# Small per-channel vectors and all constants issued from GpSimd's queue, behind a marker for the first products' input

## The chip, the cores and the metric

The kernel runs on one core of a Trainium2 chip. The metric is the device time of one launch in microseconds (us); the times shown are medians over several runs. A profiled execution gives the rows quoted below; its span reaches from the first to the last instruction.

Engines are named as the profile names them: PE is TensorE (PEld its weight loads), DVE is VectorE, ACT is ScalarE, POOL is GpSimd, SP is SyncE. A name with a q behind it (SPq, POOLq, ACTq) is the part of an engine that issues DMAs. SP and ACT issue on hardware queues, POOL on a software queue, and all of them use the same 16 DMA engines.

## The reference

256 tokens of 1024 features go through two models in a row: one hybrid layer (attention, a pooling branch, gates, a gated feed-forward with a convolution), and then two layers of latent attention and a mixture of 16 experts. Only the very start of the first one matters here:

```python
def hybrid_layer(x, norm_mix_g, w_in, b_gate, q_norm_g, k_norm_g, w_pool, pool_scale, ...):
    h = rmsnorm(x, norm_mix_g)
    proj = h @ w_in                                   # [256, 1024] @ [1024, 4096]
    q, k, v, u_pool, gate_logits = jnp.split(proj, ...)
    q = apply_partial_rotary(rmsnorm(heads(q), q_norm_g), pos)
    k = apply_partial_rotary(rmsnorm(heads(k), k_norm_g), pos)
    attn = moba_attention(q, k, heads(v))
    pooled = multiscale_pool_mixer(u_pool, w_pool, pool_scale)
    gates = jax.nn.sigmoid(gate_logits + b_gate)
    ...
    up = causal_depthwise_conv(h2 @ w_up, conv_w, conv_b)
```

The vectors q_norm_g, k_norm_g, pool_scale, b_gate, norm_ffn_g, conv_b, conv_w and their like of the later layers are the small loads that the change is about.

## The kernel before

**Products.** Every float32 matrix product is made of three products of parts: a weight or an input is split into a high and a low part (`split`, L84), the high part on ACT (L92), the low part, source minus high, on DVE (L82). A contraction step of 128 rows of w_in against 1024 of its columns is called a k here. It takes 12 matmuls of 512 columns on PE (two halves of the tokens, two halves of the columns, three products). w_in is cut into four column groups c of eight k each; the first two groups (`tm_mm`, L296 on) put tokens on partitions.

**Weight loads.** SP issues the loads of the weights in the order of their use (L137, L158 on): first the two halves of x, with the two halves of in00 between and behind them, then in01, in02, in03, in10, in11 and so on. A tile in`cu` of 1 MB (1024 KB) holds two k of group c. The tiles lie in a ring of 56 KB per partition, which holds seven of them; the eighth may be issued once the first has been split. Behind in11 SP issues 17 loads of small vectors into the tile `rows` (`add_rows`, L145; `load_rows`, L150), from 1 to 22 KB each, and only then in12.

**Lanes.** A DMA signals its landing on one of eight semaphores of its kind of queue (DMAHW0 to DMAHW7 for the hardware queues, DMASW0 to DMASW7 for POOL's). The issue of a DMA waits until the one eight before it on the same kind of queue has landed, and what stands behind it on the issuing engine waits as well.

**Constants.** POOL builds the identity for transposes, and issues 11 loads of constants, 1.7 MB in all: `at` (672 KB, what the attention needs), `bw` (q_norm_g and k_norm_g, each broadcast to 128 partitions, the rotary table, `band` of 544 KB, w_pool of 256 KB), `upb`, `cr`, `rbias` and `rw` for the experts. They don't wait for any computation, so they are issued from the first microseconds on.

**The first products.** x is transposed on PE (`x_rows`, L214), scaled and split to `hh` and `hl` (ACT L221, DVE L222), one k after the other; `keep_warm` (L97) puts transposes without use into waits of PE. ACT and DVE split the weights two k ahead of the products. After four k of the second group, `qk_norm` (L342) normalizes and rotates q and k: DVE multiplies by the row scales (L352), POOL multiplies by `qkg` (L354), DVE rotates (L359 to L364). After six k, four transposes on PE bring `rows` onto partitions (L526).

**Order.** Within an engine a planner sets the order, starting from the program's order; `tc.issue_after` holds instructions behind another one.

Of the kernel before, what the change touches and what calls it, by code (L numbers as in the profile page):

```python
# [10 lines left out]
F32 = mybir.dt.float32  # L11
# [6 lines left out]
PSUM = bass.MemoryType.PSUM  # L18

T = 256  # L20
# [10 lines left out]
# Scores of a head: 128 queries with 128 keys, then 128 queries with all 256 keys.  # L31
# [3 lines left out]
def body(tc, a, out, dbg=None, upto=None):  # L35
# [9 lines left out]
    def A(name, shape=(128, 512)):  # L45
        """One bank of PSUM."""
        return psum.tile(list(shape), F32, tag="A", name=name, bufs=4)

    def H(name, shape=(128, 2, 512)):
        """Two banks of PSUM."""  # L50
        return psum.tile(list(shape), F32, tag="H", name=name, bufs=2)
# [16 lines left out]
    def pin(i):  # L68
        """Keeps an instruction in the order of the program on its engine."""
        return tc.keep_in_program_order(i)  # L70

# [12 lines left out]
    def split(raw, shape=(1024,), eng=None, tile_=hl8, scale=1.0):  # L84
        """raw = hi + lo, both exact in float32r."""
# [11 lines left out]
    def keep_warm(n, dst):  # L97
        """Without work the clock of the tensor engine falls to half: this bridges a wait."""
# [5 lines left out]
    def after(i, col):  # L104
        """behind[i] = 1, once col is there: keeps an operation scaled by it behind col."""
        ve.tensor_scalar(behind[:, i:i + 1], col, 1.0, 1.0, op0=ALU.max, op1=ALU.min)

    def table(func, col):
        """Loads the table of a function, once col is there."""
        se.activation(warm[:, 1:2], col, func, scale=0.0, bias=epsc[0:1, 0:1])  # L110

# [29 lines left out]
    # rows of per-channel vectors, put on partitions by the tensor engine  # L141
# [3 lines left out]
    def add_rows(key, src, b, r):  # L145
        sy.dma_start(rows[n_row[b]:n_row[b] + r, b], src.rearrange("(r c) -> r c", c=128))
# [17 lines left out]
    for c in range(4):  # L164
        for u in range(4):
# [7 lines left out]
            if (c, u) == (1, 2):  # L173
                load_rows()
# [24 lines left out]
    def pre(seq, i, ahead=2, scale=1.0):  # L199
        """Keeps the splits of the units in seq up to i + ahead issued."""  # L200
# [32 lines left out]

    vec = const.tile([128, 86], F32, name="vec")
    v0 = [sum(n_row[:b]) for b in range(4)]
# [15 lines left out]
    class at:  # L251
        """What only the attention needs (and the convolution, at first): a tile for each layer."""
# [14 lines left out]
    bw = act("bw", shape=(128, 2048))  # L267
    band, wpool = (bw[:, o:o + 4 * n].rearrange("p (g c) -> p g c", g=4) for o, n in ((0, 272), (1088, 128)))
    qkg = bw[:, 1600:1728].rearrange("p (i c) -> p i c", i=2)
    cs1 = bw[:, 1728:1760].rearrange("p (t i c) -> p t i c", t=2, i=2)  # L270
    ge.dma_start(qkg[:, 0], a["q_norm_g"].partition_broadcast(128))
    ge.dma_start(qkg[:, 1], a["k_norm_g"].partition_broadcast(128))
    ge.dma_start(cs1, a["c_rot1"])
# [6 lines left out]
    # the last rows come a second time, as the router takes 32 columns at once and drops 16  # L280
# [3 lines left out]
    ge.dma_start(rw[:, KD * 16:], rsrc[:, 0])  # L284

# [7 lines left out]
    def tm_mm(c, acc, k):  # L293
# [3 lines left out]
        if c == k == 0:  # L297
            # the low part of the weights comes last
# [20 lines left out]
    for k in range(KD):  # L319
# [4 lines left out]
        if k == 3:  # L324
            # statistics of the norm, and the vectors that come later
# [52 lines left out]
    def softmax_heads(S, n_, scale, nscale, values, hi, lo):  # L378
        """Scores of two heads, a bank each, to attention outputs with features on partitions."""
# [74 lines left out]
    def fm_out(units, xh, xl, evac, then=None):  # L454
        """8 feature tiles [128, 256] in 4 banks; units: (weight name, row) per contraction tile."""
# [101 lines left out]
    def up_split(i, ss=(0, 1)):  # L557
        """hi and lo of the weights of tile pair i, gate and value."""
# [942 lines left out]
```

## Time and profile before

| What | us |
|---|---|
| Median of the timed runs (3) | 1088.08 |
| Lowest and highest of them | 1087.83, 1089.63 |
| Span of the profiled execution | 1082.4 |
| Median less that span (what lies around the span) | 5.7 |
| PE busy in the span | 1034.8 (96%) |
| DVE, ACT, POOL busy | 540.0, 427.3, 80.4 |

For the profiled execution the page gives the span and no other time, so the 5.7 us are the difference to the median of other executions. PE's busy time is modelled: its 96% say that PE has work nearly all the time, not that it runs at its peak. The chain of waits is the better guide to what sets the end, and for a change at the start of the program the time line of the first 60 us.

### The profile page before, as it was taken

How to read it: one execution, taken by the hardware profiler on the slowest of the kernel's cores; microseconds unless marked ns; L12 is line 12 of the kernel's file. 1: busy time of each engine (PE TensorE's matmuls, PEld its weight loads, DVE VectorE, ACT ScalarE, POOL GpSimd, SP SyncE). 2: the span in 40 equal slices, each digit the busy share in tenths (PEclk: the TensorE clock that was granted, in tenths of full speed). 3: DMA queues.
4: the chain of work that ended last, by engine and by line, in shares of the span. 5: the costliest groups of instructions: out<-in, count | busy, mean ns of one | idle time of the engine just before them, and what ended most of it. 6: DMA issues, size and time to landing. Idle time of an engine off the chain costs nothing.

```text
span 1082.4 us, 16579 instructions
## 1 busy us (share of the span) xinstructions
PE 1034.8 (96%) x6732; PEld 738.8 (68%) x6732; DVE 540.0 (50%) x1026; ACT 427.3 (39%) x795; POOL 80.4 (7%) x70
## 2 busy tenths in 40 slices
PE   7999999999999999999999999989999999999994
PEld 5889999999999999765343444368977534343431
DVE  3875578977777689753110111058985402011103
ACT  4766547755554565542110111156654302011111
POOL 3200021000000130010000000044000200000001
PEclk9999999999999999999999999999999999999997
DMA  9752555765443244978999999955297899999993
GB/s 320 307 183 79 208 185 173 256 203 184 156 143 142 83 159 141 352 279 311 397 394 394 396 399 395 377 201 197 79 338 283 315 381 394 398 399 400 395 387 121
DMA packets 131484, 295.08 MB, mean 273 GB/s; under 512 B 5754, under 2 KB 34744, under 8 KB 125128
## 3 DMA queue, kind: packets, MB, share of 16 engines
q1 hardware_dynamic: 130328, 290.58, 72.8%
q0 software_dynamic: 768, 2.84, 0.8%
q8 instruction: 55, 0.90, 0.3%
q10 hardware_dynamic: 304, 0.53, 0.1%
q14 instruction: 29, 0.24, 0.1%
HBM read 291.82 MB, written 2.10 MB: 272 GB/s over the span
## 4 chain that ended last, share of the span: by engine, by line
PE 79%; DVE 11%; DMA 4%; ACT 3%; issue 2%; SPq 0%; POOL 0%; DVEq 0%; ACTq 0%; POOLq 0%
PE gu L74 19%; PE up L74 12%; PE pd L74 10%; PE fm L74 7%; PE yT L74 5%; PE wo L74 5%; PE sc L74 4%; PE tm L74 4%; PE prj L74 3%; PE pg L74 3%; PE sum L74 3%; DVE hl L82 2%; PE sc L399 1%; DMA e<-in_w_down_dram 1%; DMA in<-in_w_in_dram 1%
## 5 line engine op out<-in xcount | busy, mean ns | idle before, releaser
L74 PE MATMUL gu<-e,xg 128*64 128x512 f32 x1024 | 224.2, 593 | 0.0
L74 PEld LDWEIGHTS gu<-e,xg 128*64 128x64 f32 x1024 | 72.3, 137 | 140.1 <-issue 131.5
L74 PE MATMUL up<-h2h,hl 128*128 128x256 f32 x704 | 130.5, 283 | 0.0
L1295 DVE SCALAR_TENSOR_TENSOR sg<-gu,gcol,sg 128x512 f32<-128x512 f32 x16 | 12.0, 751 | 227.5 <-PE gu L74 162.7
L74 PE MATMUL pd<-e,aT 128*64 128x512 f32 x512 | 115.9, 596 | 4.7 <-ACT aT L1305 2.7
L74 PEld LDWEIGHTS up<-h2h,hl 128*128 128x128 f32 x704 | 111.4, 192 | 0.0
L74 PE MATMUL up<-h2l,hl 128*128 128x256 f32 x352 | 99.7, 283 | 0.1
L74 PEld LDWEIGHTS pd<-e,aT 128*64 128x64 f32 x512 | 35.5, 137 | 73.5 <-issue 64.6
L74 PEld LDWEIGHTS up<-h2l,hl 128*128 128x128 f32 x352 | 67.6, 192 | 0.3 <-DVE h2l L515 0.3
L74 PE MATMUL yT<-ac,hl 128*128 128x256 f32 x528 | 67.0, 283 | 0.1
L74 PEld LDWEIGHTS yT<-ac,hl 128*128 128x128 f32 x528 | 64.9, 192 | 0.3 <-ACT ac L635 0.3
L82 DVE TENSOR_TENSOR hl<-up,hl 128x1024 fp32r<-128x1024 f32 x44 | 53.8, 1225 | 19.5 <-ACT hl L92 19.4
L1288 ACT ACTIVATE sg<-gu 128x512 f32<-128x512 f32 x16 | 9.6, 597 | 128.4 <-PE gu L74 128.4
L92 ACT ACTIVATE hl<-up 128x1024 fp32r<-128x1024 f32 x44 | 46.1, 1052 | 33.9 <-PE up L74 28.4
L1323 ACT ACTIVATE y<-pd 128x512 fp32r<-128x512 f32 x32 | 18.2, 597 | 104.1 <-PE pd L74 78.9
L82 DVE TENSOR_TENSOR y<-pd,y 128x512 fp32r<-128x512 f32 x32 | 21.3, 687 | 62.6 <-ACT y L1323 62.5
L74 PE MATMUL fm<-hh,hl 128*128 128x256 f32 x256 | 49.2, 288 | 0.9 <-ACT vu L316 0.9
L74 PE MATMUL tm<-hl,hh 128*128 128x512 f32 x128 | 41.6, 407 | 4.2 <-ACT hl L92 2.4
L1088 DVE TENSOR_SCALAR xg<-pg,vec 128x256 f32<-128x256 f32 x32 | 15.9, 538 | 59.4 <-PE sum L74 44.2
L82 DVE TENSOR_TENSOR hl<-in,hl 128x1024 fp32r<-128x1024 f32 x32 | 38.3, 1220 | 13.9 <-ACT hl L92 13.7
L1222 ACT ACTIVATE GT<-pgt 128x256 fp32r<-128x256 f32 x16 | 6.2, 384 | 95.7 <-PE pgt L1220 95.7
L74 PE MATMUL prj<-xhn,hl 128*128 128x256 f32 x208 | 40.2, 287 | 3.8 <-DVE iq L82 2.6
(354 smaller groups left out, 2052.4 us busy)
## 6 DMA issues: line engine op xcount, KB each, us to landing
e<-in_w_up_dram SPq DMA_DIRECT2D x48, 1024.0 KB
e<-in_w_down_dram SPq DMA_DIRECT2D x48, 1024.0 KB
e<-in_w_gate_dram SPq DMA_DIRECT2D x40, 1024.0 KB
e<-in_w_gate_dram SPq DMA_DIRECT2D x48, 512.0 KB
up<-in_w_up_dram SPq DMA_DIRECT2D x22, 1024.0 KB
e<-in_w_up_dram SPq DMA_DIRECT2D x32, 512.0 KB
e<-in_w_down_dram SPq DMA_DIRECT2D x32, 512.0 KB
in<-in_w_in_dram SPq DMA_DIRECT2D x15, 1024.0 KB
```

The source lines that it names most:

```text
L74: return te.matmul(o, lhsT=l, rhs=r, start=start, stop=stop, skip_group_check=True)
L82: return (eng or ve).tensor_tensor(out=dst, in0=src, in1=hi.bitcast(F32), op=ALU.subtract)
L92: se.activation(hi, raw, AF.Copy, scale=scale)
L399: te.transpose(S[:, i, 128 * b:128 * b + 128], P[:, i, 128 * b:128 * b + 128], ident)
L1088: ve.tensor_scalar(dst, src, g, b, op0=ALU.mult, op1=ALU.add)
L1222: se.activation(GTs[p], pt, AF.Copy)
L1288: se.activation(sg, psg, AF.Silu)
L1295: ve.scalar_tensor_tensor(out=sg, in0=psu, scalar=gcol[:, p:p + 1], in1=sg, op0=ALU.mult, op1=ALU.mult)
L1323: se.activation(h_, pd[c], AF.Copy)
```

## The change

`add_rows` issues on POOL (`ge`) instead of SP. A marker is put on POOL, a copy of one element of `hh` of k = 3 into the tile `warm`, and all of POOL's DMAs of constants and vectors are to be issued after it. Their order is new: q_norm_g, k_norm_g, the rotary table, then the 17 vectors of `rows`, then `at`, `band`, w_pool, `upb`, `cr`, `rbias`, `rw`. The rest of the diff takes comments away, and moves the lines that create the tile `bw` ahead of those that create `at`.

```diff
     def add_rows(key, src, b, r):
-        sy.dma_start(rows[n_row[b]:n_row[b] + r, b], src.rearrange("(r c) -> r c", c=128))
+        ge.dma_start(rows[n_row[b]:n_row[b] + r, b], src.rearrange("(r c) -> r c", c=128))
...
-            if (c, u) == (1, 2):
-                load_rows()
             load(f"in{c}{u}", w_in[u * 256:(u + 1) * 256, c * 1024:(c + 1) * 1024]
...
     x_rows(0)
 
+    mark = ge.tensor_copy(warm[0:1, 2:3], hh[0:1, 3, T - 1:].bitcast(F32))
+    behind_x = ctx.enter_context(ExitStack())
+    behind_x.enter_context(tc.issue_after(mark.ins))
+
     vec = const.tile([128, 86], F32, name="vec")
+    bw = act("bw", shape=(128, 2048))
+    band, wpool = (bw[:, o:o + 4 * n].rearrange("p (g c) -> p g c", g=4) for o, n in ((0, 272), (1088, 128)))
+    qkg = bw[:, 1600:1728].rearrange("p (i c) -> p i c", i=2)
+    cs1 = bw[:, 1728:1760].rearrange("p (t i c) -> p t i c", t=2, i=2)
+    ge.dma_start(qkg[:, 0], a["q_norm_g"].partition_broadcast(128))
+    ge.dma_start(qkg[:, 1], a["k_norm_g"].partition_broadcast(128))
+    ge.dma_start(cs1, a["c_rot1"])
+    load_rows()
...
     attention_tile(ge)
-    bw = act("bw", shape=(128, 2048))
...
-    ge.dma_start(qkg[:, 0], a["q_norm_g"].partition_broadcast(128))
-    ge.dma_start(qkg[:, 1], a["k_norm_g"].partition_broadcast(128))
-    ge.dma_start(cs1, a["c_rot1"])
     ge.dma_start(band, a["c_band"])
...
     ge.dma_start(rw[:, KD * 16:], rsrc[:, 0])
+    behind_x.close()
```

On POOL, at the start of the program and before the change, the loads of constants stand among the instructions that build the identity, and wait for nothing or, from the ninth on, for a lane:

```order
L122 CAST identb<-ident 128x128 [waits Pool_49]
L124 TENSOR_SCALAR alphaI<-ident 128x128
L248 DMA rbias<-in_router_bias_dram 128x16
L283 DMA rw<-in_router_w_dram 128x8x16
L284 DMA rw<-in_router_w_dram 128x16
L256 DMA at<-in_c_att_dram 128x1344
L271 DMA bw<-in_q_norm_g_dram 128x64
L272 DMA bw<-in_k_norm_g_dram 128x64
L273 DMA bw<-in_c_rot_dram 128x32 [waits DMASW0_49]
```

The same place with the change:

```order
L122 CAST identb<-ident 128x128 [waits Pool_49]
L124 TENSOR_SCALAR alphaI<-ident 128x128
L232 COPY warm<-hh 1x1 [waits Activation_49]
L241 DMA bw<-in_q_norm_g_dram 128x64
L242 DMA bw<-in_k_norm_g_dram 128x64
L243 DMA bw<-in_c_rot_dram 128x32
L146 DMA rows<-in_b_gate_dram 16x128
L146 DMA rows<-in_pool_scale_dram 4x128
```

The copy that waits for ACT now stands ahead of every load on POOL, and the `rows` loads have come to POOL, where they number 17 of 28 DMAs.

Further down on POOL, behind the last constants and up to its first work for `qk_norm`, before:

```order
L271 DMA bw<-in_q_norm_g_dram 128x64
L272 DMA bw<-in_k_norm_g_dram 128x64
L273 DMA bw<-in_c_rot_dram 128x32 [waits DMASW0_49]
L274 DMA bw<-in_c_band_dram 128x1088 [waits DMASW1_49]
L275 DMA bw<-in_w_pool_dram 128x4x128 [waits DMASW2_49]
L354 TENSOR_TENSOR qk<-qk,bw 128x512 [waits DMASW6_49,DVE_49,Activation_49]
```

and with the change:

```order
L146 DMA rows<-in_ln_b_dram 8x128 [waits DMASW3_49]
L266 DMA at<-in_c_att_dram 128x1344 [waits DMASW4_49]
L277 DMA bw<-in_c_band_dram 128x1088 [waits DMASW5_49]
L278 DMA bw<-in_w_pool_dram 128x4x128 [waits DMASW6_49]
L258 DMA upb<-in_c_up_dram 128x256 [waits DMASW7_49]
L258 DMA cr<-in_c_route_dram 128x100 [waits DMASW0_49]
L258 DMA rbias<-in_router_bias_dram 128x16 [waits DMASW1_49]
L286 DMA rw<-in_router_w_dram 128x8x16 [waits DMASW2_49]
L287 DMA rw<-in_router_w_dram 128x16 [waits DMASW3_49]
L358 TENSOR_TENSOR qk<-qk,bw 128x512 [waits DVE_49,Activation_49]
```

Of the 28 DMAs the last 20 now wait for a lane, in three rounds of eight, eight and four, and POOL's multiplication by `qkg` stands behind them all.

On SP, behind in11 (in_99), the first load of `rows` stood before and the weights go on now; before:

```order
L138 DMA in_97<-in_w_in_dram 128x2x1024 [waits DMAHW0_49]
L138 DMA in_99<-in_w_in_dram 128x2x1024 [waits DMAHW1_49]
L146 DMA rows<-in_b_gate_dram 16x128 [waits DMAHW2_49]
L146 DMA rows<-in_pool_scale_dram 4x128 [waits DMAHW3_49]
L146 DMA rows<-in_norm_ffn_g_dram 8x128 [waits DMAHW4_49]
```

and with the change:

```order
L138 DMA in_97<-in_w_in_dram 128x2x1024 [waits DMAHW0_49]
L138 DMA in_99<-in_w_in_dram 128x2x1024 [waits DMAHW1_49]
L138 DMA in_101<-in_w_in_dram 128x2x1024 [waits DMAHW2_49]
L138 DMA in_103<-in_w_in_dram 128x2x1024 [waits DMAHW4_49,DMAHW3_49,DVE_49]
L138 DMA in_105<-in_w_in_dram 128x2x1024 [waits DMAHW5_49,DVE_49,Activation_49]
```

in12 (in_101) follows in11 directly, 17 DMAs earlier in SP's order. On PE the order of the instructions is unchanged over the whole program. On ACT and DVE the splits of in03 to in11 and the statistics of the first norm change places with each other, behind the split of in03; from the second column group on their order is unchanged too.

## Rows read from the trace of the kernel before

**Rows 1.** The page: the chain that ended last, shares of the span by engine.
```profile
PE 79%; DVE 11%; DMA 4%; ACT 3%; issue 2%; SPq 0%; POOL 0%; DVEq 0%; ACTq 0%; POOLq 0%
```

**Rows 2.** The chain that ended last, in time: start us, us, what.
```profile
2.72 14.31 DMA in<-in_w_in_dram
...
707.85 10.78 DMA uv<-in_w_uv_dram
...
947.43 14.85 DMA e<-in_w_down_dram
```

**Rows 3.** Stretches: PE, PEld, DVE, ACT, POOL busy, PE's granted clock, DMA, GB/s.
```profile
13.50:16.00 2.50, 2.22 (x10) 1.49 (x8) 0.00 (x0) 0.00 (x0) 0.00 (x0) 1.00 1.01 124
16.00:18.00 2.00, 0.00 (x0) 0.00 (x0) 0.00 (x0) 0.94 (x1) 0.00 (x0) 1.00 0.98 390
...
19.99:23.40 3.41, 3.41 (x10) 2.64 (x9) 1.47 (x2) 0.85 (x1) 0.00 (x0) 0.50 1.02 394
23.40:36.00 12.60, 12.60 (x57) 10.43 (x56) 10.89 (x13) 11.73 (x18) 0.00 (x0) 1.00 0.54 186
```

**Rows 4.** Time line 10 to 20 us: start, us, engine, line, instruction [idle before, releaser].
```profile
10.46 1.15 ACT L92 ACTIVATE hl<-in,behind 128x1024 fp32r<-128x1024 f32 x1 [1.30 <-DMA in<-in_w_in_dram]
...
11.66 0.50 PE L74 MATMUL tm<-hl,hh 128*128 128x512 f32 x1
...
14.18 0.62 PE L74 MATMUL tm<-hl,hh 128*128 128x512 f32 x2
...
14.88 0.62 PE L74 MATMUL tm<-hl,hh 128*128 128x512 f32 x2
...
17.06 2.00 ACT L92 ACTIVATE hl<-in 128x1024 fp32r<-128x1024 f32 x2 [5.09 <-DMA in<-in_w_in_dram]
...
19.42 0.50 PE L74 MATMUL tm<-hl,hh 128*128 128x512 f32 x1 [0.76 <-DVE hl L82]
```

**Rows 5.** DMA queues, 0 to 6 us: packets, MB, share; q1 is SP's, q0 POOL's.
```profile
q1 hardware_dynamic: 462, 1.14, 59.2%
q0 software_dynamic: 31, 0.07, 3.7%
```

**Rows 6.** DMA queues, 10 to 13 us.
```profile
q0 software_dynamic: 138, 0.65, 53.4%
q1 hardware_dynamic: 134, 0.55, 46.5%
```

**Rows 7.** DMA queues, 23 to 27 us, when POOL's loads are over.
```profile
DMA packets 424, 1.64 MB, mean 411 GB/s; under 512 B 23, under 2 KB 23, under 8 KB 424
```

**Rows 8.** POOL's own time line, 0 to 60 us.
```profile
6.21 0.90 POOL L271 DMA_DIRECT2D bw<-in_q_norm_g_dram  x1
7.10 0.54 POOL L272 DMA_DIRECT2D bw<-in_k_norm_g_dram  x1
...
45.47 5.95 POOL L354 TENSOR_TENSOR qk<-qk,bw 128x512 f32<-128x512 f32 x4 [35.08 <-DVE qk L352]
```

**Rows 9.** DMA issues, 0 to 60 us: size, us from issue to landing.
```profile
bw<-in_w_pool_dram POOLq DMA_DIRECT2D x1, 256.0 KB, 13.2
...
upb<-in_c_up_dram POOLq DMA_DIRECT2D x1, 64.0 KB, 5.2
rw<-in_router_w_dram POOLq DMA_DIRECT2D x1, 64.0 KB, 7.2
```

**Rows 10.** SP's time line, 0 to 60 us.
```profile
33.65 24.87 SPq L138 DMA_DIRECT2D in<-in_w_in_dram  x10
```

**Rows 11.** DVE's time line, 0 to 70 us, and PE's at 54 us.
```profile
6.30 0.69 DVE L230 CAST hl<-in 128x1024 fp32r<-128x1024 f32 x1 [5.37 <-DMA in<-in_w_in_dram]
...
51.89 1.21 DVE L82 TENSOR_TENSOR hl<-in,hl 128x1024 fp32r<-128x1024 f32 x1
...
53.80 0.57 PE L526 MATMUL pr<-ident,rows 72*128 72x72 f32 x4
...
54.49 0.70 PE L74 MATMUL tm<-hl,hh 128*128 128x512 f32 x2
```

More of the change, by code (lines that the diff above doesn't have):

```diff
@@ L251, in body @@
     class at:
+        pass
     def attention_tile(eng):
@@ L266, in body @@
     attention_tile(ge)
-    bw = act("bw", shape=(128, 2048))
-    band, wpool = (bw[:, o:o + 4 * n].rearrange("p (g c) -> p g c", g=4) for o, n in ((0, 272), (1088, 128)))
-    qkg = bw[:, 1600:1728].rearrange("p (i c) -> p i c", i=2)
-    cs1 = bw[:, 1728:1760].rearrange("p (t i c) -> p t i c", t=2, i=2)
-    ge.dma_start(qkg[:, 0], a["q_norm_g"].partition_broadcast(128))
-    ge.dma_start(qkg[:, 1], a["k_norm_g"].partition_broadcast(128))
-    ge.dma_start(cs1, a["c_rot1"])
     ge.dma_start(band, a["c_band"])
```

## The prediction

> **What bounds the kernel now.** I read the chain of waits first. Nearly four fifths of it lie on PE, and only 4% on DMAs [rows 1]; of that the longest single piece stands at the very start, 14.31 us until 17.03 for a load of w_in [rows 2]. The change touches nothing behind the first 60 us (PE's order is the same throughout), so the question is how early PE gets into its steady run, and whether anything in those 60 us then stops it. The second view is the time line of 10 to 20 us [rows 4]. The second half of in00 reaches ACT at 10.46, after 1.30 us of waiting; in01 reaches it at 17.06, after 5.09 us of waiting. Between the two PE has one k of work, from 11.66 on, and then none: from 16 to 18 us it is busy 0.00 [rows 3]. Its steady run begins with the second product of the next k at 19.42, which waited for the low part of in01 [rows 4]. The third view is the table by stretches: from 19.99 to 23.40 the granted clock is 0.50, that is 1.2 GHz instead of 2.4, right behind the empty stretch; from 23.40 on it is 1.00 again [rows 3]. From there PE has no gap that matters; whatever it gains before 23.40 should move the whole rest.
>
> Why is in01 late? The queues tell. Until 6 us SP's queue has moved 1.14 MB and POOL's 0.07 MB [rows 5]. From 10 to 13 us POOL's queue has moved 0.65 MB and SP's 0.55 [rows 6]: the constants took more than half of the traffic just when in01 was due. From 13.5 to 16 only 124 GB/s were moved at all, against 390 behind it [rows 3] and 411 when SP is alone [rows 7]. The constants that POOL loads there are needed from 45.47 us on (`qkg`) [rows 8], or much later.
>
> **The change part by part.**
>
> *The constants leave the first 13 us.* By the end of in01 SP's queue has to move x (two times 512 KB), in00 and in01 (1024 KB each): 3.15 MB. 1.14 are there at 6 us; the other 2.01 MB at 411 GB/s [rows 7] take 4.9 us, and I add 0.35 us for the last engine and the landing: in01 at about 11.25 us instead of 17.03, and in00's second half, 1.05 MB earlier, at 8.7. Now what is late next? ACT, which was free for the split of in00 at 10.46 - 1.30 = 9.16, does it then, 1.3 us earlier [rows 4]. PE doesn't profit at once: its first product of that k at 11.66 stands behind transposes and the products of the k before, which start from in00's first half, and that lands at 6.3 either way [rows 11]. But the low part is there by then (9.16 + 1.15 + 1.23 = 11.5), so that the 12 products run through. Three take 14.88 - 14.18 = 0.70 us at most [rows 4], so twelve take 2.75: until 14.4. The split of in01 starts on ACT at 11.3 (1.05 us a k) and its low part on DVE ends by 11.3 + 1.05 + 1.2 = 13.6, before 14.4. So PE's second product of that next k comes at about 14.4 + 0.23 = 14.6 instead of 19.42: **4.8 us**.
>
> *The clock.* The stretch of 3.41 us at half clock [rows 3] does work worth 1.7 us at full clock. It stands behind 2 us without any work, and that gap closes; from 13.5 to 16 us, with PE at work for 2.22 of 2.50 us, the clock was still full [rows 3]. I take the whole gain, **1.7 us**; its lower bound is 0.
>
> *The marker.* It waits for `hh` of k = 3, which ACT writes behind the splits of in01: 11.3 + 2 x 1.05 + 0.45 = 13.9 us. Behind it on POOL stand 28 DMA issues and then the multiplication by `qkg`. The same bytes as before now run beside in02, in03 and in10. in02 is due at 11.25 + 1.05 MB / 411 GB/s = 13.8, before them. in03 would come at 16.4; with 2.5 us for a slow stretch like that of 13.5 to 16, and half of the traffic for POOL, at some 21.5. PE needs its first k at 14.4 + 4 x 2.75 = 25.4, so ACT must have it by 23.1. Cost taken: nothing; up to 1 us if in02 slips.
>
> *POOL's chain of lanes.* An issue takes 0.54 us, or 0.90 in the worst row [rows 8]. Eight issues go out at once, and each further one waits until the one eight before it has landed. With a time L from issue to landing POOL is free at 13.9 + 3 x (0.54 + L) + 4 x 0.54 = 17.7 + 3 L. The trace has small loads at 5.2 and 7.2 us, and 13.2 for one that stood behind `at` [rows 9]. In the new order the first 20 are small and have nothing large ahead of them on their queue, and the last four wait only for small ones; so I take L = 6, and POOL is free at 35.7. It is needed at 45.47 - 6.5 = 39.0. Hidden, by 3 us. If that cover goes, DVE waits with its rotation, and behind it stands the low part for k = 6 of the second group, which ended at 51.89 + 1.21 = 53.1, with PE's first use at 54.49: 1.4 us more. The transposes of `rows` at 53.80 [rows 11], then at 47.3, need the twentieth load, landed by 13.9 + 3 x (0.54 + 6) + 2.2 = 35.7.
>
> *SP without the 17 loads.* in12 was issued at 33.65 [rows 10], and comes some 27 us earlier in the queue. PE didn't wait for it before, so this gains nothing; it gives the ring a lead that pays for POOL's traffic. The identity is ready earlier too, as no DMA issue stands among its steps; in00 covers that.
>
> Sum: 4.8 + 1.7 = 6.5 us off the 1082.4 us of the profiled span. The timed median lies 5.7 us over it, and nothing in that part changes: 1088.1 - 6.5 = **1081.6 us**.
>
> **Against a rule.** The rows show two queues that share the traffic almost evenly [rows 6]. The Trainium skill, page "DMA: Bandwidth & Descriptors", section "Issuing engines are not separate DMA queues", says that DMAs of all issuing engines interleave on the same 16 DMA engines, and that spreading them saves only issue time. The trace agrees with the interleaving. By that rule alone, the bytes being the same, moving `rows` to POOL gives nothing, and the sum would be 1088; my 6.5 us come from the later time of the constants. The same page, section "SWDGE vs HWDGE vs iDMA", says that DVE can lock GpSimd out of the descriptor rings it writes. The 0.90 us issue did lie on DVE's CAST of 6.30 to 6.99, and the next one, beside a TENSOR_TENSOR, took 0.54 [rows 8, 11]; at 0.90 throughout POOL would be free at about 38, still in time.
>
> **The rivals.**
> (a) *Half the gain.* The clock falls all the same in some other stretch, or in01 comes 1 to 2 us later than 11.25 because something other than POOL's loads slowed SP's queue: 6.5 - 1.7 = 4.8, or 6.5 - 1.7 - 1.5 = 3.3 us off, so 1083.3 to 1084.8. For it: the first 6 us move 1.14 MB only, with hardly any of POOL's bytes in them. Against: at 6 us the rate is up.
> (b) *No change.* The collision only moves: the slow stretch hits in02 and in03 instead of in01, PE runs dry at k = 4, the clock falls there. in02 would have to land after 22; with SP's own loads first in line I don't see how, unless the marker comes before in01. A later DMA-bound piece could also eat the gain: 10.78 us at 707.85 and 14.85 at 947.43 [rows 2]; but those loads are issued when PE and DVE free their space, so they move with PE. 1086 to 1090.
> (c) *Slower.* POOL's lanes. PE stands still once POOL is later than 39.0 + 1.4 = 40.4, that is from L = 7.6 on. At L = 9.8 (POOL free at 47.1) the gain is used up, and from there every us of L costs 3. With 13.2 us, the slowest row [rows 9], POOL is free at 57.3, 16.9 late: 1088.1 - 6.5 + 16.9 = 1098.5. For it: the queues are full at that time, and the two broadcasts stand first. Against: 13.2 belongs to a load behind 1.2 MB on its own queue.
> That the marker fails to hold the loads is excluded by the order on POOL.
>
> **How the numbers follow.** Forecast 0.70, (a) 0.13, (b) 0.08, (c) 0.09, of which a third costs so little that it stays faster or equal. What a measurement here can tell from no change is 0.2%, 2.2 us: faster means under 1085.9. Faster: 0.70 + 0.12 + 0.01 = 0.83; same: 0.10; slower: 0.07. The range takes the forecast with 1.6 us below it (the terms at their best, in01 no bound at all), and (a) above it: 1080.0 to 1085.0; (b) and (c) stay outside.
>
> **What would show it.** In the trace after: ACT's two splits of in01 at 11 to 12 us; PE without an empty stretch from 11.66 on; the granted clock at 1.00 through 30 us; the first DMA issue on POOL at about 14; POOL's multiplication by `qkg` at 39, waiting for DVE and not for a DMA; the transposes of `rows` at 47; the whole later chain 6.5 us earlier. It is wrong if ACT waits for in02 or in03 for more than 2 us, if POOL's last issue comes after 40, or if DVE's rotation waits for POOL for longer than before.

## The result, and the profile after

| What | before | after |
|---|---|---|
| Median, us (lowest to highest) | 1088.04 (1087.83 to 1089.63) | 1079.5 (1079.11 to 1080.01) |
| Ratio, 95% interval | | 0.9932 [0.9913, 0.9951] |
| Span of the profiled execution, us | 1082.4 | 1077.6 |
| Time of that same execution, us | not given | 1079.35 |

Faster, by 8.5 us. The forecast was 1081.6 with a range from 1080.0 to 1085.0: the sign, and about three quarters of the size; the time came out half a microsecond below the range. Two later measurements of the same two programs gave 0.996 [0.9945, 0.9975] and 0.9928 [0.9907, 0.9949]; in the three groups the medians lie 8.5, 5.3 and 7.3 us apart, so the first shows the largest gain of the three. The forecast's ratio, 1081.6 / 1088.1 = 0.994, lies inside two of the three intervals. Over all 16 executions the changed kernel's median is 1079.65; over all 91 of the kernel before it is 1087.11, 7.5 us more.

Stretches of [rows 3], in the profile of after (busy us of PE, PEld, DVE, ACT, POOL, then PE's granted clock, DMA share, GB/s), with one more, from 18.5 to 20.5 us:

```profile
13.50:16.00 2.50, 2.50 (x13) 2.06 (x12) 2.42 (x4) 2.50 (x6) 1.67 (x4) 1.00 1.03 410
18.50:20.50 2.00, 2.00 (x11) 1.65 (x10) 2.00 (x4) 1.48 (x4) 0.67 (x2) 1.00 1.12 210
19.99:23.40 3.41, 3.41 (x17) 2.82 (x16) 3.41 (x5) 1.49 (x2) 1.71 (x4) 1.00 0.96 349
23.40:36.00 12.60, 12.24 (x54) 9.72 (x53) 8.59 (x9) 12.24 (x17) 9.18 (x17) 1.00 1.03 398
```

In these stretches PE has no empty time to speak of any more and no half clock (1.2 GHz instead of 2.4, which the profile writes as 0.50); the DMA engines move 410 GB/s where 124 were moved before. The slow spell has not vanished: it moved to 18.5 to 20.5 us, when the two broadcasts, issued at 14.46 and 15.23, are under way, and in02 and in03 are through. From 10 to 13 us SP's queue now has the engines to itself (packets, MB, share; compare [rows 6]):

```profile
q1 hardware_dynamic: 319, 1.24, 102.7%
```

The time line of after, with the rows that answer to [rows 4], [rows 8] and [rows 11] (start, us, engine, line, instruction, idle before and its releaser):

```profile
9.39 1.15 ACT L92 ACTIVATE hl<-in,behind 128x1024 fp32r<-128x1024 f32 x1 [0.36 <-DMA in<-in_w_in_dram]
11.90 2.01 ACT L92 ACTIVATE hl<-in 128x1024 fp32r<-128x1024 f32 x2 [0.99 <-DMA in<-in_w_in_dram]
14.33 0.18 POOL L232 COPY warm<-hh 1x1 f32<-1x1 f32 x1 [12.14 <-ACT hh L219]
14.46 0.78 POOL L241 DMA_DIRECT2D bw<-in_q_norm_g_dram  x1
14.55 0.61 PE L74 MATMUL tm<-hl,hh 128*128 128x512 f32 x2
17.27 0.61 PE L74 MATMUL tm<-hl,hh 128*128 128x512 f32 x2
33.48 0.73 PE L74 MATMUL tm<-hl,hh 128*128 128x512 f32 x2 [0.35 <-ACT qk L320]
34.55 0.55 POOL L287 DMA_DIRECT2D rw<-in_router_w_dram  x1
39.57 5.94 POOL L358 TENSOR_TENSOR qk<-qk,bw 128x512 f32<-128x512 f32 x4 [4.48 <-DVE qk L356]
...
47.90 0.57 PE L530 MATMUL pr<-ident,rows 72*128 72x72 f32 x4
```

in01 reaches ACT at 11.90 instead of 17.06. The marker passes at 14.33, POOL's last issue ends at 35.10, and POOL then waits 4.48 us for DVE: the chain of lanes is hidden. The products of the k behind in01's first start at 17.27. In the profile of before that row is

```profile
23.63 0.63 PE L74 MATMUL tm<-hl,hh 128*128 128x512 f32 x2
```

so PE is 6.36 us ahead there. At 33.48 PE waits for ACT, as it didn't before, and the lead falls from 6.39 to 5.91; the transposes of `rows` come at 47.90 instead of 53.80, 5.90 us earlier. In the chain of waits the first long piece is still a load of w_in, and a longer one than in [rows 2]:

```profile
4.50 15.80 DMA in<-in_w_in_dram
```

It is now the stream of weights itself, which ends at 20.30 with in10, at 410 GB/s in the stretch before the slow spell. Part of the 5.90 us is lost again much later in this execution. From 176 to 180 us the granted clock is 0.57, behind a spell in which PE is not quite busy:

```profile
174.00:176.00 2.00, 1.81 (x15) 1.64 (x16) 1.20 (x3) 1.28 (x3) 0.00 (x0) 1.00 0.52 211
176.00:180.00 4.00, 4.00 (x23) 4.00 (x22) 3.59 (x5) 2.70 (x4) 0.00 (x0) 0.57 0.28 72
```

PE's last products start at 1064.62 instead of 1069.01, so that 4.4 us are left of the 5.90.

### The profile page after: what moved, and what is told of

The parts are those of the page before. It is cut to its first block, busy times and chain, and to the rows that moved or that the text cites. A ratio compares the mean times of both kernels' runs of the same rounds, so it can differ in the third digit from the quotient of the medians.

```text
span 1077.6 us, 16587 instructions
## 1 busy us (share of the span) xinstructions
PE 1034.5 (96%) x6732; PEld 740.1 (69%) x6732; DVE 540.1 (50%) x1026; ACT 427.8 (40%) x795; POOL 88.9 (8%) x88
## 4 chain that ended last, share of the span: by engine, by line
PE 74%; DVE 11%; DMA 7%; ACT 4%; issue 2%; SPq 1%; POOL 0%; DVEq 0%; ACTq 0%; POOLq 0%
PE gu L74 18%; PE up L74 12%; PE pd L74 8%; PE fm L74 7%; PE yT L74 5%; PE wo L74 5%; PE sc L74 4%; PE prj L74 3%; DMA e<-in_w_down_dram 3%; PE pg L74 3%; DVE hl L82 3%; PE sum L74 2%; PE tm L74 2%; DMA in<-in_w_in_dram 1%; PE sc L403 1%
## 5 line engine op out<-in xcount | busy, mean ns | idle before, releaser
L82 DVE TENSOR_TENSOR hl<-up,hl 128x1024 fp32r<-128x1024 f32 x44 | 53.9, 1225 | 20.7 <-ACT hl L92 20.5
L74 PE MATMUL wo<-hl,oh 128*128 128x512 f32 x128 | 43.0, 408 | 0.0
## 6 DMA issues: line engine op xcount, KB each, us to landing
e<-in_w_up_dram SPq DMA_DIRECT2D x48, 1024.0 KB, 13.9
```

Source lines behind the costliest of these rows:

```text
L74: return te.matmul(o, lhsT=l, rhs=r, start=start, stop=stop, skip_group_check=True)
L82: return (eng or ve).tensor_tensor(out=dst, in0=src, in1=hi.bitcast(F32), op=ALU.subtract)
```

## The experiments

Each run was timed beside the kernel before, on one chip within each group. Spans belong to the one profiled execution of a run.

### The kernel before, again

No edit.

> The kernel before, once more, for its span beside its own time. The medians moved by 8.5 us (1088.04 to 1079.5), the two profiled spans by 4.8 (1082.4 to 1077.6), and the spans of the changed kernel's timed runs lie 1.75 us under their times. Theory 1 (an odd profile): the profiled execution of before was shorter than its timed ones, by about 4 us; then this run shows a time of 1088 with a span of about 1086, and a stretch at half clock more than the profile of before had. Theory 2 (time around the span): the kernel before loses 4 us outside its span; then this run shows 1088 with a span of about 1082.

Measured: 1087.65 us (1085.02 to 1089.95), ratio 1.0008 [0.9994, 1.0022]. The profiled execution took 1085.57 us at a span of 1083.8. Two rows of its time line:

```profile
18.38 2.00 ACT L92 ACTIVATE hl<-in 128x1024 fp32r<-128x1024 f32 x2 [6.38 <-DMA in<-in_w_in_dram]
...
55.26 0.57 PE L526 MATMUL pr<-ident,rows 72*128 72x72 f32 x4
```

and, as a stretch:

```profile
20.00:25.00 5.00, 4.54 (x11) 3.38 (x11) 2.70 (x4) 2.56 (x6) 0.00 (x0) 0.51 1.02 394
```

Here in01 is 1.3 us later than in [rows 4], PE is at half clock for 6.8 us (18.1 to 24.9) instead of 3.4, and the transposes of `rows` come 1.46 us later than in [rows 11]; the span is 1.4 us longer. What lies around a span is 1.8 us, not 5.7. Theory 2 falls. Theory 1 holds in the main: the odd profile was the prediction's, though this execution was itself quicker than the 1088 expected. Its longer stretch at half clock stands where the change works, but that is one execution: in01 reaches ACT at 17.06 in the prediction's profile, at 18.38 here, and at 16.59, 17.77 and 17.07 in the three further profiles below that leave the constants first.

### The loads of `rows` on POOL, without the marker, last

```diff
-        sy.dma_start(rows[n_row[b]:n_row[b] + r, b], src.rearrange("(r c) -> r c", c=128))
+        ge.dma_start(rows[n_row[b]:n_row[b] + r, b], src.rearrange("(r c) -> r c", c=128))
...
-            if (c, u) == (1, 2):
-                load_rows()
...
-    ge.dma_start(wpool, a["w_pool"][0].rearrange("g c d -> c g d"))
+    last_c = ge.dma_start(wpool, a["w_pool"][0].rearrange("g c d -> c g d"))
...
+    with tc.issue_after(last_c.ins):
+        load_rows()
```

> Half of the change alone: the 17 loads of rows go to POOL, behind all constants, without a marker; the constants stay in the first 10 us. Theory (early bytes): in01 is as late as before (ACT's wait until 17 us), so no change, 1087 to 1089. Rival (SP's queue: the 17 loads between in11 and in12, and SP's 6.33 us at the first of them, held the weights up): in01 at 11 to 12 us, and 1079 to 1081.

Measured: 1085.96 us (1083.58 to 1086.97), ratio 0.9991 [0.9978, 1.0003]: no difference that shows, as the theory had it (the kernel before had 1086.85 in this group). ACT's time line:

```profile
16.59 2.00 ACT L92 ACTIVATE hl<-in 128x1024 fp32r<-128x1024 f32 x2 [4.50 <-DMA in<-in_w_in_dram]
23.10 1.06 ACT L92 ACTIVATE hl<-in 128x1024 fp32r<-128x1024 f32 x1 [3.77 <-DMA in<-in_w_in_dram]
```

in01 and in02 are as late as before. The move of 17 loads to another engine's queue does nothing by itself (ratio 0.9991). That agrees with what the Trainium skill, page "DMA: Bandwidth & Descriptors", section "Issuing engines are not separate DMA queues", says of spreading DMAs over issuing engines.

### The marker alone

Against the changed kernel, the loads of `rows` go back to SP, ahead of in12; the constants stay behind the marker:

```diff
-        ge.dma_start(rows[n_row[b]:n_row[b] + r, b], src.rearrange("(r c) -> r c", c=128))
+        sy.dma_start(rows[n_row[b]:n_row[b] + r, b], src.rearrange("(r c) -> r c", c=128))
...
+            if (c, u) == (1, 2):
+                load_rows()
...
-    load_rows()
```

> The other half alone: all constants behind the marker on POOL, the 17 loads of rows on SP between in11 and in12 as before. Theory (early bytes): in01 at 11.9 us, the whole gain, 1079 to 1081. Rival (SP's queue): 1087 to 1089. If both halves are needed, something between.

Measured: 1082.13 us (1078.98 to 1084.33), ratio 0.9965 [0.9951, 0.9979]; span 1080.3. That is faster than before, but not the whole gain that the theory expected. in01 reaches ACT at 11.92, as in after. But then, in stretches as above:

```profile
30.00:32.00 2.00, 2.00 (x10) 1.65 (x10) 1.23 (x1) 2.00 (x4) 0.00 (x0) 1.00 0.02 5
...
50.00:52.00 2.00, 1.06 (x4) 0.86 (x5) 2.00 (x7) 0.00 (x0) 0.00 (x0) 0.97 1.03 403
52.00:55.30 3.30, 3.30 (x9) 2.59 (x8) 3.30 (x6) 0.05 (x1) 0.00 (x0) 0.50 0.92 302
```

and on ACT's time line:

```profile
37.02 1.06 ACT L92 ACTIVATE hl<-in 128x1024 fp32r<-128x1024 f32 x1 [3.36 <-DMA in<-in_w_in_dram]
```

From 28 to 34 us the DMA engines are nearly idle (49, 5 and 96 GB/s in three stretches of 2 us): SP goes through its 17 small loads, each behind the landing of the one eight before it, and in12 stands behind them. ACT waits 3.36 us for in12; the statistics behind it on ACT and the rotation on DVE move with it (POOL's multiplication by `qkg` starts at 43.27 instead of 39.57), and PE has a gap and then half clock. The kernel before has the same idle DMA engines, and there they cost nothing, as PE is 6 us later (a stretch of the profile of before):

```profile
30.00:32.00 2.00, 2.00 (x10) 1.68 (x9) 2.00 (x2) 1.98 (x4) 0.00 (x0) 1.00 0.01 3
```

So, by the profiles, the second part of the change has something to give only together with the first.

### The changed kernel, again (two runs)

No edit. The first was in one group with the three above.

> The changed kernel beside the others on the same chip: 1079.5, with a span 1.75 us shorter. Its profiled execution had a stretch of 3.4 us at half clock from 176 us on that the one of before did not have; if that belongs to the kernel it comes again at the same place, if to the moment it does not.

> The changed kernel unchanged. Two executions of it profiled so far have spans of 1077.6 and 1076.3 us, but five of its six timed executions beside the second took 1081.2 to 1082.6. Theory 1: the startup is the same in each execution (in01 split at 11.9 to 12.0, POOL's multiplication by qkg at 39.6), and what differs is the number of stretches at half clock later on, each 3.41 us long and worth 1.5 us: a profiled execution that takes 1081 to 1082 shows two of them more than the 1076.3 one, or one of them and a stall of PE. Rival: the startup itself is unsteady (constants or weights landing later in some executions): then POOL's multiplication by qkg comes at 41 to 44 in a slow execution and PE has a gap near 50 us, as in the run with the marker alone. Median expected by both: 1079.5 to 1081.6.

Measured: 1081.56 us (1078.07 to 1082.57), ratio 0.996 [0.9945, 0.9975], profiled at 1078.07 with a span of 1076.3; and 1079.12 us (1077.9 to 1082.64), ratio 0.9928 [0.9907, 0.9949], profiled at 1082.64 with a span of 1080.9. The start is the same in all three profiles of this kernel: in01 at 11.61 to 12.00, POOL's multiplication at 39.50 to 39.67. They differ in stretches at half clock later on. The first of the two has none until 1065.9 us, where the last products are through (every profile here ends at half clock); the stretch at 176 us in the profile of after does not come again. The second has two, behind short waits of PE in the fourth pair of experts of each layer (stretches):

```profile
584.00:586.00 2.00, 1.25 (x12) 1.15 (x11) 0.64 (x5) 1.45 (x3) 0.00 (x0) 1.00 1.06 388
586.00:588.00 2.00, 1.79 (x5) 0.69 (x6) 1.27 (x2) 0.12 (x1) 0.00 (x0) 0.61 1.09 403
...
944.00:946.00 2.00, 1.04 (x5) 0.61 (x5) 1.47 (x6) 1.29 (x3) 0.00 (x0) 0.71 1.05 387
```

Theory 1 holds, its rival falls. Set side by side, the two profiles' products lie within 0.2 us of each other from 40 to 584 us; behind the first stretch (3.41 us) the slower one is 1.5 us late, behind the second, twice as long, 4.5, and that is nearly the whole difference of their spans, 4.6. The executions that were only timed agree: each has its mean granted clock beside it, and of the 12 here those at 0.995 took 1077.9 to 1078.6 us, those at 0.993 1081.2 to 1081.6, those at 0.991 1082.6.

The short wait of PE ahead of a stretch is not enough to bring it. At 176 us the first of the two profiles has the same spell as the profile of after, and the full clock behind it:

```profile
174.00:176.00 2.00, 1.81 (x15) 1.64 (x16) 1.18 (x3) 1.19 (x2) 0.00 (x0) 1.00 0.61 248
176.00:178.00 2.00, 2.00 (x19) 2.00 (x18) 2.00 (x4) 1.97 (x4) 0.00 (x0) 1.00 0.03 8
```

### The loads of `rows` on SP, but further back

Against the run with the marker alone:

```diff
-            if (c, u) == (1, 2):
+            if (c, u) == (2, 0):
                 load_rows()
```

> The marker as in the changed kernel, but the 17 loads of `rows` on SP, ahead of in20 instead of ahead of in12 (and not on POOL). In the run with the marker alone the DMA engines moved 5 to 96 GB/s from 28 to 34 us while SP went through these loads, and ACT waited 3.36 us for in12, which made the rotation on DVE 3.6 us late and gave PE a gap of 2 us and a half-clock stretch near 50 us. Theory 1 (the loads hurt only because in12 stands behind them while the ring still has free space): behind in13 they find the ring full, ACT does not wait for in12, POOL's multiplication by qkg starts at 39.6 as in the changed kernel and no half-clock stretch comes at 50 us; span 1076 to 1078 if undisturbed, median 1080 to 1082. Rival: loads of vectors on SP cost wherever they stand, then a wait for in20 or later replaces that for in12 and the median is 1082 or more.

Measured: 1079.35 us (1079.06 to 1081.56), ratio 0.9939 [0.9917, 0.9961], a little under the 1080 to 1082 of theory 1; the 1082 or more of its rival did not come. POOL's multiplication comes at 38.62, and PE has no gap before 56 us; ACT does wait 3.35 us for a later load of w_in, but no product was waiting for that (time lines of POOL and ACT):

```profile
38.62 5.93 POOL L359 TENSOR_TENSOR qk<-qk,bw 128x512 f32<-128x512 f32 x4 [14.93 <-DVE qk L357]
43.47 2.15 ACT L92 ACTIVATE hl<-in 128x1024 fp32r<-128x1024 f32 x2 [3.35 <-DMA in<-in_w_in_dram]
```

By the profiles it is the place in SP's order that matters, not the queue. The times alone don't separate the two: in their groups the marker alone had 0.9965, this one 0.9939, and the changed kernel 0.996 and 0.9928.

### The change without the marker

```diff
-    mark = ge.tensor_copy(warm[0:1, 2:3], hh[0:1, 3, T - 1:].bitcast(F32))
-    behind_x = ctx.enter_context(ExitStack())
-    behind_x.enter_context(tc.issue_after(mark.ins))
...
-    behind_x.close()
```

> The changed kernel without the marker: POOL issues the two broadcasts, the rotation table, the 17 loads of `rows` and then the large constants as early as it gets to them. Theory 1 (the bytes of the large constants ahead of in01 are what cost the time): these stand behind 20 small loads, of which only eight can be on their way at once, so that few of their bytes move before in01; in01 is split at 12 to 14 us instead of 17 to 18.4, the gain is 3 to 5 us: 1082 to 1084. Theory 2 (the two broadcasts slow all transfers down while they run, 2.5 us at 124 GB/s in the kernel before): these now run before 10 us, in00 or in01 come some 2.5 us later than with the marker, in01 at 14.5 or later; 1084 to 1086. No difference between the kernel before and this one (1087) would say that the marker alone does the work.

Measured: 1081.01 us (1077.99 to 1082.53), ratio 0.9938 [0.9916, 0.9961]; with the marker it was 0.9928 [0.9907, 0.9949] in this group, so the two can't be told apart. The start is the same too: the transposes of `rows` come at 47.91. POOL now issues from the first microseconds on, but the planner has put the loads of `rows` and the broadcasts first, and the large constants stand behind their lanes (time line of POOL, then ACT):

```profile
9.87 0.57 POOL L237 DMA_DIRECT2D bw<-in_q_norm_g_dram  x1 [0.99 <-DMA rows<-in_norm_ffn_g_dram]
...
15.06 0.51 POOL L146 DMA_DIRECT2D rows<-in_ln_g_dram  x1 [0.66 <-DMA bw<-in_q_norm_g_dram]
17.08 0.50 POOL L146 DMA_DIRECT2D rows<-in_ln_b_dram  x1 [1.52 <-DMA bw<-in_k_norm_g_dram]
18.02 0.54 POOL L262 DMA_DIRECT2D at<-in_c_att_dram  x1 [0.44 <-DMA bw<-in_c_rot_dram]
```

```profile
12.35 2.01 ACT L92 ACTIVATE hl<-in 128x1024 fp32r<-128x1024 f32 x2 [1.30 <-DMA in<-in_w_in_dram]
```

The DMA queues from 10 to 13 us, and a stretch:

```profile
q1 hardware_dynamic: 296, 1.15, 98.9%
q0 software_dynamic: 127, 0.03, 4.6%
```

```profile
14.00:16.00 2.00, 2.00 (x10) 1.62 (x9) 1.92 (x4) 1.08 (x3) 0.91 (x2) 1.00 1.03 185
```

`at` goes out at 18.02. From 10 to 13 us POOL's queue moves 0.03 MB and SP's 1.15. So the lanes of twenty small loads hold the bytes of the large constants back as well as the marker does, and in01 comes early, as theory 1 had it. Theory 2 is not refuted by that. The two broadcasts go out at 9.87 and 10.44 but land only just ahead of the issues at 15.06 and 17.08 that wait for their lanes, and the slow spell (185 GB/s) lies at 14 to 16 us: it, too, has moved behind in01. No run keeps the broadcasts ahead of in01 and moves the large constants alone. An estimate from [rows 3] and [rows 7]: from 13.5 to 16 us of before 124 GB/s were moved, and 411 when SP was alone, so 2.5 x (1 - 124 / 411) = 1.7 us; that would be the share of the slow spell in the 5.2 us by which the change brings in01 forward, and the bytes of the constants would have the rest.

### The kernel before, with PE's gap filled (two tries)

The first put 26 transposes into the gap, the second eight products that add nothing to an open sum (each is two instructions of the profile); the edit of the second:

```diff
+    def fill(n, dst):
+        for i in range(n):
+            mm(dst[0:64, 0:256], ident[0:64, 64:128], x_tm[0:64, 0, 0:256], False, False)
...
+        if c == 0 and k == 2:
+            fill(6, acc[0][0])
...
+                if c == 0 and k == 2 and tt == h == 0:
+                    fill(2, acc[0][0])
```

> The kernel before with 26 transposes more on PE (x of the first k again, into the same place, 0.13 us each): 18 ahead of the first product of the k that waits for in01, 8 between that product and the next, which fill most of the gap of 2.44 and 0.76 us there. in01 is as late as before. Theory 1 (the half clock is a consequence of the gap, and a term of its own): no half-clock stretch between 15 and 30 us, the products of the next k start no earlier, and the rest comes 1.5 to 3.4 us earlier: 1084 to 1086. Rival (the stretch has nothing to do with the gap): it stays, and the time is that of before or up to 1 us more.

> The first try to fill PE's gap in the kernel before put transposes into a tile that DVE still read; they waited until 20.71 us and the gap grew from 2.4 to 4 us. Here the filling is eight products 64x256 of the identity's zero block with x, added to the open sum (adding nothing): six ahead of the first product that waits for in01, two between it and the next. They wait for nothing but PE. in01 is split at 17 to 18.4 as before. Theory 1 (the half clock follows the gap): no half-clock stretch between 15 and 30 us in this profile, and the median 1.5 to 3 us under that of the kernel before: 1083.5 to 1085.5 where before is 1087. Rival (half the array at work is not enough, or the stretch has another cause): a half-clock stretch of 3.41 or 6.83 us all the same, the time within 1 us of before.

The first did not fill it: its transposes wrote a tile that DVE still had to read, waited until 20.71 us, and made the gap longer; 1090.01 us, ratio 1.0032 [1.0017, 1.0047], with 6.8 us at half clock. The second filled the gap: 1088.32 us (1085.0 to 1090.51), ratio 1.0014 [1.0, 1.0027]. Its time line (PE and ACT), and then its stretches:

```profile
15.98 2.80 PE L74 MATMUL tm<-x_tm,ident 64*64 64x256 f32 x12
...
20.14 0.50 PE L74 MATMUL tm<-hl,hh 128*128 128x512 f32 x1
23.46 1.06 ACT L92 ACTIVATE hl<-in 128x1024 fp32r<-128x1024 f32 x1 [3.66 <-DMA in<-in_w_in_dram]
...
26.59 0.50 PE L74 MATMUL tm<-hl,hh 128*128 128x512 f32 x1 [0.69 <-DVE hl L82]
38.53 0.74 PE L74 MATMUL tm<-hl,hh 128*128 128x512 f32 x2 [0.96 <-ACT qk L324]
```

```profile
18.00:20.00 2.00, 2.00 (x9) 0.88 (x7) 1.75 (x3) 1.80 (x4) 0.00 (x0) 1.00 1.03 416
20.00:22.00 2.00, 2.00 (x9) 1.54 (x9) 1.48 (x2) 0.00 (x0) 0.00 (x0) 1.00 1.02 371
```

The half clock is gone from the start, so it did follow the gap: the profiles with a gap of 1.9 to 4 us there have it, the others don't. But this filling gained nothing. It took longer than the gap, so that the second product of the k comes at 20.14, 0.72 us later than the 19.42 of [rows 4]. One k later PE is 0.84 us ahead of the profile of before, so 1.6 us were saved on the way. Then it waits for in02, which is late too (26.59), and for ACT's evictions (38.53 and 41.20), and by the transposes of `rows` (55.63) it is later than in both profiles of the kernel before (53.80 and 55.26). Theory 1 was right on the cause of the stretch and on its size up to that point, and wrong on what would be left of it. What a filling that costs nothing would give is not shown.

### The constants later still

Eight fills of a 128x2048 tile on POOL between marker and first load (1.83 us each). Eight loads of `rows` go out between the fills, from 16.25 on; the first broadcast goes out at 32.83 instead of 14.46, and POOL's last issue ends at 46.24 instead of 35.10.

> The changed kernel with eight fills of a 128x2048 tile on POOL between the marker and the first load, so that the whole chain of loads starts and ends later by their length D (which the trace gives; some 8 to 20 us by the 1.48 us that POOL takes for a multiplication of 128x512). In the changed kernel POOL's last issue ends at 35.1 to 35.6 and DVE is ready for the multiplication by qkg at 39.6. Theory (rival (c) of the prediction, with its price): POOL is late by D - 4.2 us, DVE's rotation by as much, and PE loses that less some 1.4 us, with 1.5 us more for a half-clock stretch behind the gap. At D = 10: PE has a gap of 4.4 us between 47 and 56 us and the time is 1079.5 + 4.4 + 1.5 = 1085; at D = 16: 1091, slower than the kernel before. Rival: the loads are needed much later than I think and the time stays at 1079 to 1082.

Measured: 1089.16 us (1088.44 to 1092.96), ratio 1.0032 [1.0019, 1.0045]. Slower than before, as rival (c) would have it, but not by its mechanism (time line of PE and POOL):

```profile
40.24 1.22 PE L74 MATMUL tm<-hl,hh 128*128 128x512 f32 x2 [8.48 <-ACT qk L322]
...
49.16 5.95 POOL L360 TENSOR_TENSOR qk<-qk,bw 128x512 f32<-128x512 f32 x4 [2.93 <-DVE qk L358]
```

POOL waits for DVE here, not DVE for POOL. The planner knew of the fills and put the statistics of the first norm behind the splits of the second column group, so that PE stood still for 8.48 us; the clock was at half from 34 to 44 us. The price of a POOL that is really late was not measured, and rival (c) is not tested by this. What the trace of after shows is the cover, 4.48 us.

### Two variants that go further

The changed kernel with PE's short waits in the fourth pair of experts filled, and the same with `rows` on SP ahead of in20:

```diff
                 pt = A("pact", (128, 4, 128))
+                if p == 3:
+                    keep_warm(4, pt[:, 0])
...
                     slot_gates(p // 2 + 1)
+                    if p == 3:
+                        keep_warm(6, pt[:, 0])
```

> The changed kernel with ten transposes of the identity more per layer in the fourth of the eight expert pairs, where PE waits 0.67 and 0.96 us (583.1 to 586.2 and 942.3 to 945.4 us): four ahead of the transposes of the activation, six behind the products of the gates. Three of five profiles of kernels that start like the changed one show a half-clock stretch of 3.41 us behind the first of these places, two of them one of 3.41 or 6.83 us behind the second. Theory: these stretches follow the short waits; with the waits filled none comes at 586 and 945, the profile shows at most the one at 176, and the median falls by 1 to 2 us, to 1077.5 to 1078.5, with less scatter. Rival: the filling takes as much time as it saves, or the stretches move elsewhere: 1079 to 1081.

> The two variants that start or run best, together: the marker for the constants on POOL, the 17 loads of `rows` on SP ahead of in20, and the ten transposes more per layer in the fourth expert pair. The first alone had PE's products 0.6 to 0.9 us earlier than the changed kernel from 31 us on and a median of 1079.35; the second alone 1078.98, with five executions within 1.2 us. Theory: the two add up, as they lie 550 us apart: 1077.5 to 1078.5, no half-clock stretch at 586 and 945 us. Rival: what the loads of `rows` save at the start is used up by a later load that PE waits for: 1078.5 to 1079.5, no faster than either.

Measured: 1078.98 us (1078.55 to 1079.75), ratio 0.993 [0.9915, 0.9946]; and 1078.17 us (1077.89 to 1078.7), ratio 0.9907 [0.989, 0.9924]. The second median lies in the range of its theory, the first between those of theory and rival. Neither profile has a half-clock stretch at 586 or 945; two of the three profiles of the changed kernel have none there either, so that the filling did it is not shown. Both have one that none of the others shows, from 716 to 720 us, behind a spell with PE at 2.44 of 4.00 us. Of the second kernel, in stretches:

```profile
712.00:716.00 4.00, 2.44 (x20) 2.00 (x18) 2.79 (x4) 3.94 (x8) 2.36 (x1) 1.00 0.06 26
716.00:720.00 4.00, 4.00 (x24) 4.00 (x24) 2.42 (x6) 3.14 (x7) 1.65 (x3) 0.62 0.01 4
```

Both beat the kernel before. Their intervals overlap with those of the changed kernel, so that they beat it too is not shown. That the two edits add up is not shown either: the second kernel's start is no earlier than after's.

## Why the prediction was right, and where it was off

**in01 and the start: right.** Forecast 11.25 us for in01 and 14.6 for the second product of the next k; measured 11.90 and 14.78, so 4.64 us gained of the 4.8. The 0.65 us of in01 did not reach PE: as worked out there, the low part was ready (14.22) before PE had done the k before (14.55). That POOL's loads ahead of in01 were the cause, and not the move of `rows`, is shown by the loads of `rows` moved alone (no gain, in01 at 16.59), the marker alone (in01 at 11.92) and the change without the marker (in01 at 12.35, a time that can't be told from that of the change). What is argued only is how the 5.2 us by which in01 comes earlier divide between the bytes of the large constants and the slow spell at the broadcasts.

**The clock: size right, but it hangs on the loads.** 1.72 us came on top of the 4.64 within one k (23.63 - 17.27 = 6.36), against 1.7 forecast, and the stretch from 19.99 to 23.40 is at 1.00. The sum treated it as a term of its own. In the filled kernel a saving of that size was there too, and went to waits for in02 and for ACT. Here it stayed because in02 and in03 came early as well: ACT did not wait for in02, and for in03 only 0.20 us. "From there PE has no gap that matters" was nearly right: a wait for ACT at 33.48 took 0.48 us of the lead, which no term of the sum held.

**The marker and POOL's chain: right.** 13.9 forecast, 14.33 measured; L = 6 taken, 4.7 to 7.2 us measured for the first 20 loads; POOL free at 35.7 forecast, 35.10 measured; needed at 39.0 forecast, 39.57 measured. The 4.7 to 7.2 us are the medians of each kind of load, so the cover was as thin as forecast, some 4 us. Rivals (b) and (c) did not come: the slow spell found in02 and in03 landed, and POOL waits for DVE. Of rival (a) one part came in the profile of after: the clock fell in another stretch, at 176 us, and took 1.5 us. The long issues of 0.90 us don't need a busy DVE: in the profile of before, the load of `rw` took 0.91 us at 4.25, when DVE had nothing to do until 6.30.

**`rows` away from SP: wrongly priced at nothing, by the profiles.** "PE didn't wait for it before, so this gains nothing" read the cover of before, and the other half of the change takes that cover away. With `rows` left ahead of in12, the profile loses 3.6 us by the last product against the run of the changed kernel in the same group (spans 1080.3 and 1076.3), and 3.4 of them come between 48 and 56 us. In the medians of that group it is 0.6 us (1082.13 against 1081.56), too little to resolve; the scatter of later stretches lies over it.

**The base of the sum: misread.** "The timed median lies 5.7 us over it, and nothing in that part changes" is wrong. What lies around the span is 1.74 to 1.91 us in every execution where both are given (1085.57 and 1083.8; 1079.35 and 1077.6). So the profiled execution of before took about 1082.4 + 1.8 = 1084.2 us, and the other 3.9 us were the difference between a quick execution and the median one: of 87 later executions of this kernel, six took no more than 1084.3. The sum took a gain from a quick execution off a median. What is certain is that in that execution the two terms were sized well: 6.5 us forecast, 6.39 reached, 5.90 left at 53.80 and 4.4 at the end.

Why the medians lie further apart, 7.5 us over all executions and 5.3 to 8.5 by group, is not shown. Two things are seen. The start varies: the second profile of before is 1.46 us later at the transposes of `rows`, and against it the change gains 55.26 - 47.90 = 7.36 us. But in01 at 18.38 there is the latest of the five profiles with early constants, so this needn't be the usual start. And stretches at half clock later on vary in both kernels, at 1.5 us for 3.41 us. That the 7.36 us come close to the 7.5 is therefore no proof, and that the time came out within 2.1 us of the forecast is in part luck.

## What to carry to other kernels

In this kernel constants that nobody needed for 30 us still cost when they were issued first: count the bytes of all queues ahead of the first weights, look for slow spells there as well, and put what isn't needed behind something that waits, be it a marker or only a row of small loads with lanes. Price each part of a change against the timeline with the other parts in place; a wait that is covered today may be the next one due. And before a sum of a few microseconds is hung on one profiled execution, compare its own time with the median: if it is a quick one, ask where the median one loses the difference, and profile it more than once.

## What the runs showed of the hardware

- Stretches at half clock, 3.41 or 6.83 us long, come behind short spells with PE not quite busy (1.04 to 1.81 of 2.00 us in the rows above), in some executions and not in others of the same program, at 176, 586 or 945 us; the same spell at 174 us stands in another execution with the full clock behind it. Each 3.41 us cost about 1.5 us. Between two profiles of the changed kernel they make 4.5 us of a difference of 4.6.
- Loads of a 256-byte row to 128 partitions use up DMA time out of proportion: from 18.5 to 20.5 us of after POOL's 0.07 MB took 61.4% of the engines' time, SP's 0.35 MB 50.8%, and only 210 GB/s were moved. The slow spell goes with them: 124 GB/s from 13.5 to 16 us in before, 185 from 14 to 16 without the marker, 210 from 18.5 to 20.5 in after.
- Seventeen small loads in a row on one queue leave the DMA engines all but idle: 3 to 5 GB/s from 30 to 32 us, in the kernel before and with the marker alone.
